# Delta-rule values transposed by VectorE and a trip through DRAM instead of by TensorE, and low parts of weights by an adding DMA, in a one-core decoder layer

## The chip, the core and the metric

The kernel runs on one core of a Trainium2 chip. The metric is the time of one execution on the device, in microseconds. Three runs of the kernel before took 1606.45, 1606.53 and 1606.76 us; the median is 1606.53 us.

## The reference

One layer of a decoder with 512 tokens of width 1024, all in float32: a half-weighted SwiGLU block (inner width 2816), a mixer, a second half-weighted SwiGLU block, and a final RMSNorm. The mixer projects its normalised input with one wide matrix and gives the columns to two branches: an HGRN2 branch (8 heads, columns called Q, F and B here) and a gated DeltaNet branch (8 key heads `k` and `q`, 16 value heads `v`, output gates `z`, and a few columns `D` for decays). The branches are projected back, merged by two gates (`t`), and projected once more. The change is in the DeltaNet branch, whose core is, for every value head and every chunk:

```python
cq, ck, cv = split(silu(causal_short_conv(concat(gq, gk, gv))))   # 4 taps along the tokens
u = T @ (v * beta[..., None])          # T: inverse of a unit lower triangular matrix of the chunk
w = T @ (kb * exp(gam)[..., None])
v_new = u_c - w_c @ S
o = (q_c * exp(gam_c)) @ S + qk_c @ v_new
S = S * exp(g_end) + k_to_end.T @ v_new
```

The convolution runs along the tokens, so its output is made with channels on the partitions; the recurrence multiplies `v` by matrices over tokens, so it wants tokens on the partitions. Between the two, each value head's block of 128 channels by 512 tokens has to be turned.

## The kernel before

**Tiling.** Activations lie transposed, channels on the 128 partitions and 512 tokens along the free axis. The kernel's chunk is 128 tokens, so there are NT = 4 chunks. Two value heads share a key head, and the kernel works on such pairs, `u` = 0 to 7.

**Precise products from pairs.** Weights and activations are split into a high part that TensorE's float32r format holds and a low remainder, and every product is three matmuls (`mm3`, L189 to L191: high by high, high by low, low by high). A weight slab is 128 x 512. In the mixer, SP loads it into one of three buffers `raw` (L1712), ScalarE copies it to `whi` (rounding, L1754), VectorE subtracts that from `raw` to give `wlo` (L1756), and TensorE uses both for four blocks of rows. There are six pairs of `whi` and `wlo` (WB = 6), three to each of two lanes that take turns. In the two SwiGLU blocks some slabs are done differently (L333 and L334): ScalarE writes minus the high part into `wlo`, and a DMA that GpSimd issues loads the weight from DRAM a second time and adds it into `wlo`.

**Stages.** The first SwiGLU block runs to about 360 us of the span, the mixer from there to about 1250, the second SwiGLU block to the end. Within the mixer the HGRN2 heads come first, then the DeltaNet pairs, and last a closing product `wbg` of the DeltaNet outputs, with the merge and the output projection.

**A planned order.** In the mixer, the order of instructions on every engine is fixed when the program is built. Each piece of work is a Python generator (a thread). It yields what it wants next: an engine for a reckoned time (`V(512)` is VectorE for 0.21 + 0.512 us, `A` is ScalarE, `T_` is TensorE, `S` is 0.4 us of SP), a pause (`lag`), a buffer (`get`), or events of other threads (`on`). The class `Desk` plays these against each other in reckoned time and writes down the instructions in the order that comes out; of the threads that are ready, the lowest rank goes first. Pieces marked `Patient` stand aside for up to 4 us (WAIT) while the dense products run. On the chip each engine then runs its list strictly in order, and waits where data or a buffer are not ready.

**The threads that matter here.**

- `loader` picks the next 128 columns to project from the list DENSE, as far as their buffers are free (`choose`), and loads their slabs. At most CONVS = 7 convolutions may be under way. If no column may be loaded it takes one of the 16 gate tiles `t`, as long as more than two are left; else it asks SP again after 0.5 us of reckoned time.
- `maker` turns a raw slab into its pair; `product` multiplies, in the order of loading.
- `conv` takes a projected k, q or v tile, scales it, applies the four taps (three steps of VectorE) and SiLU, and writes the result. For a value head that is L1113 into a buffer `vb`, channels on partitions.
- `g_w`, for each value head: four transposes of 128 x 128 on TensorE into a PSUM tile `ptv` (L1251), then a multiplication by per-token factors on VectorE (L1253) back into `vb`, now tokens on partitions.
- `g_n` and `g_b`: the pair's lower triangular blocks (eight products on VectorE, L1204); these go through DRAM to GpSimd, which inverts the 32 x 32 diagonal blocks in 31 dependent steps of two instructions (L1240, L1241).
- `g_inv` completes the inverse on TensorE; `g_rec` is the recurrence over the four chunks (L1374 to L1414), then normalisation, a transposition back (L1445) and the output gate. Pair `u` needs the inverse of `u`, and buffers that pair `u - 2` or an earlier one gives back.
- `operand` and, for the last two heads, the end of `g_rec` (L1458, L1460) split the outputs into pairs for the closing product, which uses heads 0 to 3 first and heads 12 to 15 last.

Of the kernel before, what the change touches and what calls it, by code (L numbers as in the profile page):

```python
# [8 lines left out]
F32 = mybir.dt.float32  # L9
# [3 lines left out]
ALU = mybir.AluOpType  # L13
# [3 lines left out]
P = 128  # L17
T = 512
# [30 lines left out]
STAY = (15,)  # L49
CONVS = 7  # L50
SLACK = 0.8
LAG = dict(raw=3.5, gb=6.5, nb=6, m=7, out=5, back=6)
EASE = 2.5
LANES = {"a": 2, "b": 2, "d": 1, "e": 1}

# [632 lines left out]
def mixer(tc, mp, e):  # L688
# [8 lines left out]
    def ps(name, lane="d"):  # L697
        return psc.tile([P, T], F32, tag="p" + lane, name=name, bufs=LANES[lane])

    def v3(ap, a):  # L700
        return ap.rearrange("p (a b) -> p a b", a=a)

    def bc(ap, n):

        return ap.unsqueeze(2).to_broadcast([ap.shape[0], ap.shape[1], n])
# [385 lines left out]
    def conv(k, i, pt, out, n):  # L1091

        yield "get", "ta", 2
        yield *V(512), 1
        ci = ta("ci", (P, T + 32))[:, :T + 3]
        dve.memset(ci[:, :3], 0.0)
        dve.tensor_tensor(ci[:, 3:], pt, rbc, op=ALU.mult)
        D.put("mm")
        wc = [cs[:, C_CV + 4 * i + j:C_CV + 4 * i + j + 1] for j in range(4)]
        yield A(512)  # L1100
        y = ta("cy")
        act.activation(y, ci[:, :T], AF.Copy, scale=wc[0])
        for j in range(1, 4):
            yield V(550)
            dve.scalar_tensor_tensor(y, ci[:, j:j + T], wc[j], y, op0=ALU.mult, op1=ALU.add)
        yield A(512)
        th = ci[:, :T]
        act.activation(th, y, AF.Tanh, scale=0.5)
        a, b = (v3(th, n), v3(y, n)) if n else (th, y)
        if k[0] in "qk" and k[1] > 3:  # L1110
            yield "on", ("K", k[1] - 4)
        yield V(512)
        dve.scalar_tensor_tensor(out, a, 1.0, b, op0=ALU.add, op1=ALU.mult)  # L1113
        D.put("ta", 2)
        D.fire(k)

    def g_e(u, st):

# [124 lines left out]

    def g_w(u, i, st):
        yield "on", ("v", 2 * u + i), ("C", u)
        yield "get", "e", 1
        vb = G["vb"][u % 3 * 2 + i]
        yield T_(Patient(.5))
        pt = ps("ptv", "e")
        for c in range(NT):  # L1250
            pe.transpose(pt[:, c * P:(c + 1) * P], vb[:, c], ident)  # L1251
        yield V(512)
        dve.tensor_tensor(vb, v3(pt, NT), bc(st["c2"][:, :, i], P), op=ALU.mult)  # L1253
        D.put("e")
        D.fire(("W", u, i))

    def g_inv(u, st):
# [75 lines left out]
    def g_rec(u, st):  # L1333
        yield "on", ("I", u), ("W", u, 0), ("W", u, 1), ("N", u), *([("R", u - 2)] if u > 1 else []), \
            *(["more"] if u else [("x", 0), ("we", 0), ("w", 0)])
        kq, kn, at, ut, sm = (st[k] for k in ("kq", "kn", "at", "ut", "sm"))
        vb = G["vb"][u % 3 * 2:u % 3 * 2 + 2]
        hd2 = [slice(i * P, (i + 1) * P) for i in range(2)]
        we, w, x = (G[n][u % 2] for n in ("we", "w", "x"))
        s = None  # L1340
# [27 lines left out]
        for c in range(NT):  # L1368
            pk = None
            if c > 0:  # L1370
                yield "get", "a", 1
                yield T_(.88)
                pk = ps("pks", "a")
                pe.matmul(pk[:, :256], kq[:, c, 0], s, start=True, stop=True)  # L1374
                pe.matmul(pk[:, 256:], kq[:, c, 1], s, start=True, stop=True)
                for i in range(2):
                    yield V(150)
                    dve.scalar_tensor_tensor(x[:, hd2[i]], pk[:, hd2[i]], st["c1"][:, c, i:i + 1], vb[i][:, c],
                                             op0=ALU.mult, op1=ALU.add)
                xs = [x[:, :P], x[:, P:]]  # L1380
            else:
                xs = [vb[0][:, c], vb[1][:, c]]
            yield "get", "b", 1
            yield T_(.46)
            pw = ps("pw", "b")
            for i in range(2):
                pe.matmul(pw[:, hd2[i]], ut[:, 4 * i + c], xs[i], start=True, stop=True)  # L1387
            D.start((2, u, c, 0), values(c, pw))
            if c < NT - 1:
                for i in range(2):  # L1390
                    yield V(150)
                    dve.tensor_scalar(we[:, hd2[i]], pw[:, hd2[i]], ek[:, c, 2 * u + i:2 * u + i + 1], None,
                                      op0=ALU.mult)
            yield "on", ("w", u, c)
            D.put("b")

            yield "get", "b", 1
            yield T_(.9)
            po = ps("pog", "b")
            if c < NT - 1:  # L1400
                pe.matmul(po[:, :256], kn[:, c], we, start=True, stop=True)
            for i in range(2):
                pe.matmul(po[:, 256 + i * P:256 + (i + 1) * P], at[i][:, c], w[:, hd2[i]], start=True, stop=True)  # L1403
            D.start((2, u, c, 1), outputs(c, po, pk))
            if c < NT - 1:
                yield "get", "s", 1
                s2 = places["s"]("s", (P, 256))
                if c == 0:
                    yield V(256)
                    dve.tensor_copy(s2, po[:, :256])  # L1410
                else:
# [284 lines left out]
    def loader():  # L1696
        n = 0
        while todo or gates:
            yield "get", "raw", 1
            x = choose()  # L1700
            while x is None:
                yield "use", "SP", 0.5
                x = choose()
            line.append(x)
            D.fire(("f", x))
            D.fire(("line", len(line)))
            for q, src in enumerate(weights(*x)):
                if q:
                    yield "get", "raw", 1
                yield S  # L1710
                raw = wp.tile([P, 512], F32, tag="raw", name="raw", bufs=RB)
                sp.dma_start(raw, src)  # L1712
                D.start((1, n), maker((x, q), raw))
                n += 1
        for d, q in wbgs:
            yield "get", "raw", 1
            yield S
            raw = wp.tile([P, 512], F32, tag="raw", name="raw", bufs=RB)
            sp.dma_start(raw, wbg[d][:, q * 512:(q + 1) * 512])
            D.start((1, n), maker((("m", d), q), raw))  # L1720
            n += 1

    def extra(n):
# [1 line left out]
        ab = op[4 + n]("wx", (P, 2, T), F32R)  # L1725
        return ab[:, 0], ab[:, 1]

    def maker(key, raw):
        yield "lag", LAG["raw"]
        (k, i), q = key  # L1730
        if k == "D":
# [20 lines left out]
            yield A(512)  # L1752
            lo, hi = e["pair"]()
        act.copy(hi, raw)  # L1754
        yield V(512)
        dve.tensor_tensor(lo, raw, hi.bitcast(F32), op=ALU.subtract)  # L1756
        D.put("raw")
        made[key] = hi, lo
        yield "lag", .4
        D.fire(("slab", key))  # L1760

    def product():
        for n in range(len(todo) + len(gates) + len(line)):
# [215 lines left out]
```

## Time and profile before

| | |
|---|---|
| median of three runs | 1606.53 us |
| profiled execution, span from first to last instruction | 1604.7 us |
| PE (TensorE matmul) busy | 1593.7 us, 99% |
| DVE (VectorE) busy | 1145.7 us, 71% |
| ACT (ScalarE) busy | 831.0 us, 52% |
| POOL (GpSimd) busy | 408.8 us, 25% |
| moved by DMA | 204.91 MB, 128 GB/s on average |
| of that, queue of GpSimd's DMAs | 26.22 MB |

The page gives the profiled execution's span and not its whole time; the median of the runs is 1.8 us above that span. PEld is TensorE's loading of weights, which overlaps its matmuls, and SPq is the queue of SP's DMA issues. In a row of a group, the names after the operation are output and inputs (buffer numbers left out), then shapes, then the count; behind the bar stand the busy time and the mean of one in ns, and after the next bar the idle time in front of it and what ended it. In a row of the timeline the first number is the start, the second the duration, both in us; brackets give the idle time before and what ended it.

### The profile page before, as it was taken

The numbers are of one execution on the slowest core, as the hardware profiler recorded it, in microseconds if no ns is written. First come the engines' busy times: TensorE is split into PE (matmuls) and PEld (weight loads), VectorE is DVE, ScalarE is ACT, GpSimd is POOL, SyncE is SP. The second block draws the span as 40 slices with busy tenths as digits, with TensorE's granted clock in tenths as the row PEclk, the third lists the DMA queues.
The fourth block names the chain that finished last, engine by engine and source line by source line (L and its number), as shares of the span: only waits on it lengthen the run. The fifth ranks groups of instructions, "written<-read, shape, count | busy, mean of one in ns | idle before, by whom it ended". The sixth has DMA issues, their size and how long they took to land.

```text
span 1604.7 us, 29242 instructions
## 1 busy us (share of the span) xinstructions
PE 1593.7 (99%) x10672; PEld 1386.3 (86%) x10672; DVE 1145.7 (71%) x2259; ACT 831.0 (52%) x1872; POOL 408.8 (25%) x725
## 2 busy tenths in 40 slices
PE   9999999999999999999999999999999999999997
PEld 8999998888888888888888888888888899999887
DVE  6888785447787778668788888765545788878433
ACT  5766674332434345456665665554324666667222
POOL 0211212001221221156545556600001121121001
PEclk9999999999999999999999999999999999999998
DMA  5766863332312322443242334445543586686333
GB/s 187 168 162 156 181 160 103 113 117 86 106 47 68 86 92 87 137 135 104 93 125 80 119 107 129 134 136 186 164 142 128 140 183 158 154 187 146 92 91 117
DMA packets 121824, 204.91 MB, mean 128 GB/s; under 512 B 21184, under 2 KB 27072, under 8 KB 121680
## 3 DMA queue, kind: packets, MB, share of 16 engines
q1 hardware_dynamic: 104688, 172.40, 34.3%
q0 software_dynamic: 14400, 26.22, 10.2%
q10 hardware_dynamic: 2592, 4.42, 1.0%
q8 instruction: 84, 1.38, 0.4%
q14 instruction: 60, 0.49, 0.1%
HBM read 188.02 MB, written 14.97 MB: 126 GB/s over the span
## 4 chain that ended last, share of the span: by engine, by line
PE 91%; DMA 3%; issue 3%; DVE 2%; ACT 0%; POOL 0%; POOLq 0%; SPq 0%; DVEq 0%; ACTq 0%
PE pmm L189 19%; PE pmm L191 19%; PE pmm L190 19%; PE px L191 6%; PE px L190 6%; PE px L189 6%; DMA wlo<-w1a 2%; PE pnat L189 2%; PE pnat L191 2%; PE pnat L190 2%; PE pgq L1189 1%; PE pw L1387 1%; PE pog L1403 1%; PE pl L974 1%; PE pd L917 1%
## 5 line engine op out<-in xcount | busy, mean ns | idle before, releaser
L189 PE MATMUL pmm<-uh,whi 128*128 128x512 f32 x879 | 361.3, 411 | 0.0
L191 PE MATMUL pmm<-uh,wlo 128*128 128x512 f32 x879 | 343.0, 390 | 0.0
L190 PE MATMUL pmm<-ul,whi 128*128 128x512 f32 x879 | 341.9, 389 | 0.0
L191 PE MATMUL px<-xs,wlo 128*128 128x256 f32 x1008 | 285.7, 283 | 1.3 <-DMA wlo<-w1a 0.7
L190 PE MATMUL px<-xs,whi 128*128 128x256 f32 x1008 | 285.2, 283 | 0.0
L189 PE MATMUL px<-xs,whi 128*128 128x256 f32 x1008 | 285.2, 283 | 0.0
L1754 ACT CAST whi<-raw 128x512 fp32r<-128x512 f32 x226 | 140.2, 621 | 242.7 <-PE pmm L190 195.2
L1756 DVE TENSOR_TENSOR wlo<-raw,whi 128x512 fp32r<-128x512 f32 x226 | 158.3, 702 | 118.2 <-ACT whi L1754 116.2
L191 PEld LDWEIGHTS pmm<-uh,wlo 128*128 128x128 f32 x879 | 165.0, 188 | 36.1 <-DVE wlo L607 0.2
L191 PEld LDWEIGHTS px<-xs,wlo 128*128 128x128 f32 x1008 | 193.5, 192 | 2.1 <-DMA wlo<-w1a 1.1
L189 PEld LDWEIGHTS px<-xs,whi 128*128 128x128 f32 x1008 | 193.5, 192 | 0.1
L190 PEld LDWEIGHTS px<-xs,whi 128*128 128x128 f32 x1008 | 193.5, 192 | 0.1
L189 PEld LDWEIGHTS pmm<-uh,whi 128*128 128x128 f32 x879 | 165.5, 188 | 30.4
L190 PEld LDWEIGHTS pmm<-ul,whi 128*128 128x128 f32 x879 | 165.7, 189 | 29.5 <-DVE ul L216 0.2
L329 ACT CAST whi<-sw 128x512 fp32r<-128x512 f32 x144 | 87.6, 613 | 92.8 <-DVE sw L366 72.6
L308 DVE TENSOR_TENSOR wlo<-raw,whi 128x512 fp32r<-128x512 f32 x100 | 77.7, 788 | 76.7 <-ACT whi L329 76.3
L329 ACT CAST whi<-raw 128x512 fp32r<-128x512 f32 x104 | 61.2, 592 | 125.6 <-PE pmm L190 92.8
L227 POOL TENSOR_TENSOR acc<-acc,sqt 128x512 f32<-128x512 f32 x18 | 23.4, 1302 | 319.8 <-ACT sqt L225 319.8
L308 DVE TENSOR_TENSOR wlo<-sw,whi 128x512 fp32r<-128x512 f32 x144 | 98.0, 681 | 0.0
L329 ACT CAST whi<-rw 128x512 fp32r<-128x512 f32 (+1 forms) x130 | 79.6, 613 | 26.6 <-PE px L190 13.4
L190 PE MATMUL pmm<-xs,whi 128*128 128x512 f32 (+1 forms) x238 | 89.7, 377 | 0.1
L189 PE MATMUL pmm<-xs,whi 128*128 128x512 f32 (+1 forms) x238 | 89.8, 377 | 0.0
(476 smaller groups left out, 3223.5 us busy)
## 6 DMA issues: line engine op xcount, KB each, us to landing
raw<-wt SPq DMA_DIRECT2D x160, 256.0 KB
rw<-w1b SPq DMA_DIRECT2D x80, 256.0 KB
rw<-w1a SPq DMA_DIRECT2D x74, 256.0 KB
wlo<-w1b POOLq DMA_DIRECT2D x53, 256.0 KB, 4.8
wlo<-w1a POOLq DMA_DIRECT2D x47, 256.0 KB, 5.0
raw<-w2b SPq DMA_DIRECT2D x41, 256.0 KB
raw<-w2a SPq DMA_DIRECT2D x36, 256.0 KB
raw<-wn SPq DMA_DIRECT2D x32, 256.0 KB
```

The lines of the kernel that those rows point to most:

```text
L189: pe.matmul(pt, ah, bh, start=first, stop=False)
L190: pe.matmul(pt, ah, bl, start=False, stop=False)
L191: pe.matmul(pt, al, bh, start=False, stop=last)
L227: add.tensor_tensor(acc, acc, s, op=ALU.add)
L308: dve.tensor_tensor(lo, x, hi.bitcast(F32), op=ALU.subtract)
L329: act.copy(hi, x)
L917: pe.matmul(pd[c // 2][:, (c % 2) * 192:(c % 2) * 192 + 192], ke[:, c * P:(c + 1) * P], qq[:, c], start=True, stop=True)
L974: pe.matmul(pl_[s0:s0 + 32, c * 16:(c + 1) * 16], ke[:, c * P + s0:c * P + s0 + 32], qv[:, c, r, :, 1], start=True, stop=True)
L1189: pe.matmul(pq[:, (c % 2) * 256:(c % 2) * 256 + 256], kq[:, c, 0], kq[:, c].rearrange("p a b -> p (a b)"), start=True, stop=True)
L1387: pe.matmul(pw[:, hd2[i]], ut[:, 4 * i + c], xs[i], start=True, stop=True)
L1754: act.copy(hi, raw)
L1756: dve.tensor_tensor(lo, raw, hi.bitcast(F32), op=ALU.subtract)
```

## The change

Two things change in the mixer.

**Turning the values.** For a value head, `conv` now writes its result to its own scratch tile `y`, and VectorE transposes it within blocks of 32 x 32 (`turn`) into the scratch tile `th`. `bounce` writes that tile to DRAM (256 KB) and reads it back in four transfers of 64 KB, one per 32 channels, each of which places the blocks so that tokens lie on partitions in `vb`. `g_w` then only multiplies, in place and from SBUF. In `vb` the columns are now ordered by block of 32 channels, then chunk, then channel, and `g_rec` reads them through a rearranged view. The two scratch tiles are given back at different times.

**Folded slabs.** Of every two slabs of a k, q, v or z tile, the second gets its low part as the SwiGLU blocks do: ScalarE writes the negated high part, and a DMA issued by GpSimd loads the weight again and adds it. The buffer `raw` is given back before that DMA.

Beside these, a loader that finds nothing to load asks again after 0.2 us of reckoned time rather than 0.5, behind all other work for SP.

```diff
-LAG = dict(raw=3.5, gb=6.5, nb=6, m=7, out=5, back=6)
+LAG = dict(raw=3.5, gb=6.5, nb=6, m=7, out=5, back=6, turn=2.5, fold=4.5)
...
         yield V(512)
-        dve.scalar_tensor_tensor(out, a, 1.0, b, op0=ALU.add, op1=ALU.mult)
-        D.put("ta", 2)
+        if n:
+            dve.scalar_tensor_tensor(out, a, 1.0, b, op0=ALU.add, op1=ALU.mult)
+            D.put("ta", 2)
+        else:
+            dve.scalar_tensor_tensor(y, a, 1.0, b, op0=ALU.add, op1=ALU.mult)
+            yield V(512)
+            turn(th, y)
+            D.put("ta")
+            yield from bounce(f"vn{i}", th, out, "ta")
         D.fire(k)
+
+    def turn(out, x):
+
+        dve.transpose(out.rearrange("p (f c j) -> p c f j", f=4, c=NT), x)
+
+    def bounce(name, x, out, tag=None):
+
+        yield S
+        scr = dr.tile([P, T], F32, name=name)
+        sp.dma_start(scr, x)
+        yield "lag", LAG["turn"]
+        if tag:
+            D.put(tag)
+        for f in range(4):
+            yield S
+            sp.dma_start(out[32 * f:32 * f + 32].rearrange("p (r a) -> p r a", r=4),
+                         scr.rearrange("(r i) (f a) -> f i r a", i=32, f=4)[f])
+        yield "lag", LAG["turn"]
...
     def g_w(u, i, st):
         yield "on", ("v", 2 * u + i), ("C", u)
-        yield "get", "e", 1
-        vb = G["vb"][u % 3 * 2 + i]
-        yield T_(Patient(.5))
-        pt = ps("ptv", "e")
-        for c in range(NT):
-            pe.transpose(pt[:, c * P:(c + 1) * P], vb[:, c], ident)
+        vb = G["vb"][u % 3 * 2 + i].rearrange("p r (c j) -> p r c j", c=NT)
         yield V(512)
-        dve.tensor_tensor(vb, v3(pt, NT), bc(st["c2"][:, :, i], P), op=ALU.mult)
-        D.put("e")
+        dve.tensor_tensor(vb, vb, st["c2"][:, :, i].unsqueeze(1).unsqueeze(3).to_broadcast([P, 4, NT, 32]), op=ALU.mult)
         D.fire(("W", u, i))
...
-        vb = G["vb"][u % 3 * 2:u % 3 * 2 + 2]
+        vb = [x.rearrange("p r (c j) -> p c r j", c=NT) for x in G["vb"][u % 3 * 2:u % 3 * 2 + 2]]
...
-                    dve.scalar_tensor_tensor(x[:, hd2[i]], pk[:, hd2[i]], st["c1"][:, c, i:i + 1], vb[i][:, c],
+                    dve.scalar_tensor_tensor(v3(x[:, hd2[i]], 4), v3(pk[:, hd2[i]], 4), st["c1"][:, c, i:i + 1], vb[i][:, c],
                                              op0=ALU.mult, op1=ALU.add)
...
             while x is None:
-                yield "use", "SP", 0.5
+                yield "use", "SP", 0.2, 20
                 x = choose()
...
         act.copy(hi, raw)
-        yield V(512)
-        dve.tensor_tensor(lo, raw, hi.bitcast(F32), op=ALU.subtract)
-        D.put("raw")
+        if folded(k, q):
+            yield A(512)
+            act.mul(lo, hi.bitcast(F32), -1.0)
+            D.put("raw")
+            yield "use", "POOL", .9
+            pool.dma_start(lo, src, accum_op=ALU.add)
+            yield "lag", LAG["fold"]
+        else:
+            yield V(512)
+            dve.tensor_tensor(lo, raw, hi.bitcast(F32), op=ALU.subtract)
+            D.put("raw")
+            yield "lag", .4
         made[key] = hi, lo
-        yield "lag", .4
         D.fire(("slab", key))
+
+    def folded(k, q):
+        return k in 'kqvz' and q % 2
```

Left out are the lines that hand the slab's source to `maker`.

More of the change, by code (lines that the diff above doesn't have):

```diff
@@ L1712, in loader @@
                 sp.dma_start(raw, src)
-                D.start((1, n), maker((x, q), raw))
+                D.start((1, n), maker((x, q), raw, src))
                 n += 1
@@ L1719, in loader @@
             sp.dma_start(raw, wbg[d][:, q * 512:(q + 1) * 512])
-            D.start((1, n), maker((("m", d), q), raw))
+            D.start((1, n), maker((("m", d), q), raw, wbg[d][:, q * 512:(q + 1) * 512]))
             n += 1
@@ L1726, in extra, with maker @@
         return ab[:, 0], ab[:, 1]
-    def maker(key, raw):
+    def maker(key, raw, src=None):
         yield "lag", LAG["raw"]
```

## The prediction

> **What bounds the kernel now.** I read the header and the engine table of the page, then TensorE's list of waits, then the busy time of each engine by stretch, and last the order of starts on TensorE around a transpose that goes.
>
> ```profile
> span 1604.7 us, 29242 instructions
> ...
> PE 1593.7 (99%) x10672; PEld 1386.3 (86%) x10672; DVE 1145.7 (71%) x2259; ACT 831.0 (52%) x1872; POOL 408.8 (25%) x725
> ```
> ```profile
> PE pbc L654 <- POOL rl L252: 1.1, 1, 1.1
> ```
> ```profile
> 100.00:200.00 100.00, 100.00 (x836) 100.00 (x835) 82.02 (x145) 63.74 (x123) 20.18 (x24) 1.00 0.73 167
> 900.00:950.00 50.00, 50.00 (x330) 41.52 (x329) 43.74 (x102) 33.35 (x102) 29.95 (x67) 1.00 0.37 116
> ```
>
> TensorE is busy for 1593.7 of 1604.7 us. Its list of waits (total, times, longest) has five rows, this one the longest, and none lies in the mixer. In the stretches (length, PE, PEld, DVE, ACT, POOL, clock, DMA share, GB/s) the delta rule's 900 to 950 has TensorE at 50 of 50, VectorE at 43.7, ScalarE at 33.4, GpSimd at 30.0. Since the end of a matmul is modelled, a wait could hide in it; so I look at starts:
>
> ```profile
> 667.80 0.39 PE L191 MATMUL pmm<-oh,wlo 128*128 128x512 f32 x1
> ...
> 670.52 0.39 PE L191 MATMUL pmm<-oh,wlo 128*128 128x512 f32 x1
> 670.75 0.60 PE L1251 MATMUL ptv<-sq,gvb 128*128 128x128 f32 x4
> 671.11 0.48 PE L189 MATMUL pmm<-oh,whi 128*128 128x512 f32 x1
> 671.42 0.39 PE L190 MATMUL pmm<-oh,whi 128*128 128x512 f32 x1
> ```
>
> Twelve steps lie between 667.80 and 670.52: 0.227 us from start to start, though each matmul "lasts" 0.39. The queue is really dense, and the cost of a matmul is its step. **TensorE's own work sets the time**; another engine matters only where it makes TensorE wait.
>
> **The change, part by part.** *The transposes.*
>
> ```profile
> L1251 PE MATMUL ptv<-sq,gvb x48: 270/272/330, 670.8 to 1027.7; 128*128 128x128 f32 x48
> L1251 PE MATMUL ptv<-sq,x x16: 272/272/328, 779.1 to 967.7; 128*128 128x128 f32 x16
> ```
>
> 64 transposes go, four for each of 16 heads. By durations that would be 64 x 0.272 = 17.4 us, but they overlap their neighbours. By starts, 670.52 to 671.42 holds two dense steps (0.453) and one head's four transposes: 0.90 - 0.453 = 0.447 us. Rounded down to 0.44, for heads that stand beside other small matmuls: 16 x 0.44 = **7.0 us less on TensorE**. The first chunk's L1387 now reads its values in runs of 32 with gaps: 16 small matmuls, at nothing because count and shape stay; at some 2 us in all if the gaps cost half of a 0.27 us matmul.
>
> *VectorE, ScalarE, GpSimd.* The rows give count, busy time and mean ns, or least, median and most ns.
>
> ```profile
> L1756 DVE TENSOR_TENSOR wlo<-raw,whi 128x512 fp32r<-128x512 f32 x221 | 155.0, 702 | 112.5 <-ACT whi L1754 110.5 <-PE pw L1387 0.6
> ...
> L1253 DVE TENSOR_TENSOR gvb<-ptv,sm 128x512 f32<-128x512 f32 x12 | 8.2, 681 | 2.0 <-PE ptv L1251 2.0
> ...
> L1272 DVE STREAM_TRANSPOSE h<-x 32x256 f32<-32x256 f32 x8 | 3.5, 435 | 0.2
> ...
> L1265 DVE STREAM_TRANSPOSE x<-gln 128x256 f32<-128x256 f32 x3 | 2.1, 701 | 0.0
> ```
> ```profile
> L333 ACT ACTIVATE wlo<-whi x100: 631/632/637, 39.4 to 1462.6; 128x512 fp32r<-128x512 f32 x100
> ```
> ```profile
> L334 POOL DMA_DIRECT2D wlo<-w1b x53: 853/862/929, 1256.4 to 1463.8; - x53
> ...
> DMA to landing us min/median/max: 3.8/4.8/7.8
> ```
>
> The k, q, v and z columns are 48 tiles of two slabs, so 48 subtractions leave VectorE: 48 x 0.702 = 33.7 us. Sixteen transposes of 128x512 come, a size without a row. The 256-wide ones take 0.435 (L1272) or 0.701 (L1265, scattered), so I bound it by 0.44 and twice 0.70, and take twice 0.435, as the new one reads in order like L1272: 14 us, at most 22. The multiplication stays at about 0.7 (L1253 from PSUM, L1756 from SBUF alone). VectorE is relieved by 20 us, at least 11. ScalarE gets 48 x 0.632 = 30 us, GpSimd 48 x 0.862 = 41 us, over some 400 us in which the stretch above leaves them a third and two fifths free.
>
> The Trainium skill ("VectorE: DVE Perf Modes", Rules for kernel authors) speaks against this part: a 128x128 transpose belongs on TensorE if PSUM will do as its destination. By duration the trace agrees, 0.45 us a head against 0.87 and a DMA trip; by that rule the sum would be a loss, which is rival C below.
>
> Does the longer way of a slab show?
>
> ```profile
> ACT whi L1754 <- PE pmm L190: 108.5, 101, 3.4
> ```
>
> ScalarE's slab copy mostly waits for a buffer that TensorE gives back, so the six pairs are full, and a new slab is wanted five slabs later: 5 x 12 x 0.227 = 13.6 us. Copy 0.62, negation 0.63 and landing 4.8 make 6.1 us, 9.1 with the longest landing: hidden, at nothing. Without this cover each folded slab would cost about its 6 us, against 1.3 of a plain one.
>
> *The trip through DRAM.* SP issues five more transfers per head, 80 in all; its first read waits for the write, and the loads of raw slabs stand behind it, for which ScalarE waits. The plan allows 2.5 us; the nearest row, a 256 KB transfer with addition, has 3.8 to 7.8. So SP stands 1 to 5 us per head, and I take 2. The multiplication waits for the reads in the same way, with the recurrence's small VectorE steps behind it; VectorE's idle 6 us in 50 and the 20 us of relief take up 16 x 2 us. Traffic grows by 80 x 256 KB = 21 MB, 52 GB/s on top of 116; at 167 (100 to 200 above) TensorE is still full. All this I cost at nothing; its other end is rival C.
>
> *The end of the mixer*, where the cover is thin. The chain on GpSimd (L1240, L1241) and the recurrence behind it must be over before the closing product needs the last head.
>
> ```profile
> 1010.25 0.26 POOL L1240 TENSOR_TENSOR fm<-gfs,gln 128x31 f32<-128x31 f32 x1 [11.77 <-DMA gln<-hmask]
> ...
> 1040.90 0.20 POOL L1241 TENSOR_TENSOR gln<-gln,fm 128x8 f32<-128x8 f32 x1
> ```
> ```profile
> 1123.11 0.60 PE L1445 MATMUL pto<-sq,on 128*128 128x128 f32 x4
> ...
> 1131.73 0.39 PE L189 MATMUL pmm<-uh,whi 128*128 128x512 f32 x1
> ```
> ```profile
> 1125.47 0.69 DVE L1460 TENSOR_TENSOR ul<-on,uh 128x512 fp32r<-128x512 f32 x1
> ```
>
> Head 15's operand is written at 1126.2. Counted from the start of the closing product, TensorE's matmul at 1131.73 is the first to use it: 5.6 us to spare. With 7.0 us less work TensorE arrives at 1124.7, so **what is late next** is this operand, by 1.4 us, if the recurrence ends where it does. Does it? One fold comes per tile, about every 8 us, so four fall into a GpSimd chain of 31 us (1010.25 to 1041.1): +3.4 us a chain. Against that:
>
> ```profile
> 674.87 0.25 POOL L1240 TENSOR_TENSOR fm<-gfs,gft 128x30 f32<-128x30 f32 x1
> ...
> 675.55 0.58 POOL L1240 TENSOR_TENSOR fm<-gfs,gft 128x29 f32<-128x29 f32 x1
> ```
> ```profile
> 927.93 0.78 DVE L1204 SCALAR_TENSOR_TENSOR gn<-gm,sm,x 128x128 f32<-128x128 f32 x2
> ...
> 946.83 1.48 DVE L1204 SCALAR_TENSOR_TENSOR gn<-gm,sm,x 128x128 f32<-128x128 f32 x5
> ```
>
> The 0.58 is an instruction that ran beside a slab subtraction on VectorE, the 0.25 one that did not: four subtractions fewer give a chain back some 1.3 us. (The Trainium skill, "GPSIMD Engine Reference", Key points, has GpSimd share its SBUF interfaces with VectorE and contend with instructions of two SBUF inputs; the trace agrees, 0.25 to 0.58.) And the eight products that feed the next chain are split by 18 us of other VectorE work, of which the relief, 20 us for eight pairs of heads, gives back 2.5 a pair. So +3.4 - 1.3 - 2.5: about nothing. I take an unmoved end, with 7 us earlier and 15 later as bounds.
>
> **The sum**: 1604.7 - 7.0 + 1.4 = 1599.1 for the profiled execution. The page gives its span only; the runs' median is 1606.53, so 1.8 us lie around the span: 1600.9.
>
> **The rivals.**
>
> *B, GpSimd becomes the bound, slower.* A fold holds GpSimd for 0.86 us and also while it waits for ScalarE's negation, which stands behind copies that wait up to 3.4 us for TensorE. The last two chains, of 31 us like the one above, carry some 7 folds. If each holds GpSimd for 1.9 us, less the 0.33 of a subtraction not met, the end moves by 7 x 1.57 = 11 us and the closing product waits it out: 1600.9 + 11 = 1612. It is slower by 0.2% from 1.6 us a fold (7 x 1.27 = 9). For it: GpSimd carries the only long serial chain, and each fold makes it meet an engine that TensorE paces. Against it: the plan puts each issue after the time it reckons for the negation.
>
> *C, slabs come late.* The two values of a pair bounce close together; then SP may stand 2 x 5 us, and with a folded slab's 9.1 that is 19 against 13.6 of cover: 5.5 us for each of 8 pairs, 44 at worst. I price a quarter: 1600.9 + 11 = 1612. It is slower by 0.2% once SP stands for 4.3 us a trip (8 x (8.6 + 6.1 - 13.6) = 9). For it: the load of the next slab stands in the same queue as the bounce. Against it: the median landing of 4.8 leaves 2.3 us a trip. (The Trainium skill, "DMA: Bandwidth & Descriptors", Anatomy of one DMA, has a wait sit on the issuing sequencer before dispatch; by that, all behind it stands too, which no run here shows yet.)
>
> *D, no net change.* If the recurrence is already the bound, TensorE's 7 us turn into a wait at the closing product: 1606 to 1607. For it: the loader takes a gate tile only when no projection may be loaded, and did so amid the delta rule:
>
> ```profile
> 997.14 0.68 DVE L1479 TENSOR_TENSOR tg<-pmm,rbc 128x512 f32<-128x512 f32 x1
> ```
>
> Against it: 5.6 us to spare.
>
> **How the numbers follow.** 0.2%, 3.2 us, is about what a measurement of this kernel can tell from no change. Forecast (1599 to 1603.3): 0.54. D: 0.17. B: 0.17. C: 0.12. So faster 0.54, same 0.17, slower 0.29. The likeliest is 1600.9. Downwards the range needs the full 7.0 with no stall and 1 us of unknowns, 1598.5; upwards it takes in D and the prices of B and C, to 1613, which leaves out their worse half, some 0.15. The forecast's own range is 1598.5 to 1603.3.
>
> **What would show it.** No L1251 in the trace, and TensorE's starts still 0.227 apart between 650 and 1030; a wait of 1 to 2 us of TensorE on the last operands of the closing product; VectorE some 20 us less busy, ScalarE 30 more. B would show GpSimd waiting on the negation and its chains over 36 us; C TensorE waiting on slabs and SP on the bounce's write; D a closing wait near 7 us. Wrong altogether if TensorE waits in the middle of the delta rule for something that stands in no row here.

## The result, and the profile after

The changed kernel took 1613.99 us (median of six runs, 1610.8 to 1618.68) against 1606.51 of the kernel before in the same session: the ratio is 1.0047, 95% interval 1.0036 to 1.0058. It is slower by half a per cent, where 1600.9 had been forecast. The profiled execution took 1610.8 us, the lowest of the six, and has a span of 1609.0; it lies 3.2 us below the median, and what follows is read from it.

The profile of the changed kernel, header and engine table:

```profile
span 1609.0 us, 29388 instructions
...
PE 1590.0 (99%) x10608; PEld 1378.9 (86%) x10608; DVE 1128.4 (70%) x2227; ACT 859.7 (53%) x1920; POOL 453.7 (28%) x773
```

The forecast sums of the engines came nearly true: 64 matmuls fewer, VectorE 17 us less busy, ScalarE 29 and GpSimd 45 more. Where is the time? The mixer lies between two broadcasts on TensorE. Before, they start at 363.27 and 1251.22, 887.95 us apart; after, the timeline of TensorE has:

```profile
362.76 1.05 PE L1881 MATMUL pbc<-sq,rcol 128*128 128x128 f32 x8
...
1254.93 1.05 PE L243 MATMUL pbc<-sq,rcol 128*128 128x128 f32 x8
```

That is 892.17 us: 4.2 more where 7.0 less were expected, so 11.2 us are lost inside the mixer, and the rest of the span is as it was. TensorE's list of waits after (total, times, longest) has five rows in the mixer, where the kernel before has none. The two costliest stand first:

```profile
PE pgq L1214 <- DVE gqm L1220: 3.5, 2, 3.2
PE pks L1393 <- DVE s L1433: 2.1, 1, 2.1
PE pbc L654 <- POOL rl L252: 1.1, 1, 1.1
...
PE pog L1420 <- DVE gwe L1411: 1.0, 2, 0.6
```

Both wait for small steps of VectorE, a masked product of 0.4 us and an update of the state of 0.35. Why were they late? VectorE's list and SP's, from 640 to 1060 us, rows with the trip through DRAM:

```profile
DVE gvb L1273 <- DMA gvb<-vn: 26.2, 10, 5.5
DVE x L1273 <- DMA x<-vn: 1.7, 2, 1.4
```
```profile
SPq L1138 <- DMA vn<-ci: 20.0, 10, 4.0
```

VectorE stood 28 us in front of the multiplication (L1273), and SP 20 us in front of the reads. One such place, on SP, VectorE and TensorE in turn:

```profile
672.05 0.43 SPq L1132 DMA_DIRECT2D vn<-ci  x1
...
675.51 1.74 SPq L1138 DMA_DIRECT2D gvb<-vn  x4
```
```profile
675.92 0.42 DVE L1218 TENSOR_TENSOR gm<-pgq,sq 128x256 f32<-128x256 f32 x1
679.05 0.69 DVE L1273 TENSOR_TENSOR gvb<-gvb,sm 128x512 f32<-128x512 f32 x1 [2.71 <-DMA gvb<-vn]
679.66 0.42 DVE L1220 TENSOR_TENSOR gqm<-pgq,sq 128x256 f32<-128x256 f32 x1
```
```profile
676.66 0.39 PE L191 MATMUL pmm<-oh,wlo 128*128 128x512 f32 x1
680.23 2.04 PE L1214 MATMUL pgq<-h 128*128 128x256 f32 x4 [3.18 <-DVE gqm L1220]
681.71 0.99 PE L189 MATMUL pmm<-oh,whi 128*128 128x512 f32 x1
682.50 0.63 PE L190 MATMUL pmm<-oh,whi 128*128 128x512 f32 x1
```

The write goes out at 672.05, the reads at 675.51, the multiplication runs at 679.05: 7.0 us, where the plan allows 2.5 for each half. L1220, whose input had long been there, stands behind the multiplication; it frees the PSUM tile that TensorE needs at L1214, and all dense products of the queue stand behind that. The chain of waits of the changed kernel has the same two pieces:

```profile
672.05 3.40 DMA vn<-ci
...
676.82 2.11 DMA gvb<-vn
679.05 0.12 DVE gvb L1273
```

The wait is dearer than it is listed. Until 683.70 the matmuls step by 0.79, 0.42, 0.43 and 0.35 us in place of 0.227, and L1214's four take 1.48 (680.23 to 681.71) in place of some 0.67: 1.9 us more. The windows (length, PE, PEld, DVE, ACT, POOL, clock, DMA share, GB/s) show why:

```profile
660.00:676.00 16.00, 16.00 (x76) 13.26 (x75) 6.90 (x15) 8.26 (x26) 4.28 (x9) 1.00 0.62 190
676.00:680.00 4.00, 1.04 (x5) 0.53 (x3) 1.29 (x5) 0.62 (x1) 3.22 (x11) 1.00 0.68 205
680.00:682.00 2.00, 1.77 (x5) 1.51 (x5) 0.68 (x2) 0.00 (x0) 1.76 (x4) 0.54 0.41 124
682.00:684.00 2.00, 2.00 (x7) 1.56 (x6) 1.69 (x6) 0.00 (x0) 0.31 (x1) 0.60 0.36 122
684.00:690.00 6.00, 6.00 (x28) 4.98 (x27) 3.16 (x8) 2.35 (x4) 3.19 (x7) 1.00 0.57 127
```

After the idle time the granted clock is 0.54 and 0.60, and 1.00 again from 684. By starts, against dense steps, this one place costs some 5.2 us, the one at 1010 (2.13 us listed, behind a stand of 4.94 us of VectorE) 2.4, and five smaller ones (0.3 to 0.6 us listed) some 2.9 together: 10.5 of the 11.2 us. Of the five, one, at 880 us, is right behind a stand of VectorE for the trip (2.65 us); two lie beside the HGRN2 heads, before any value head is turned.

### The profile page after: what moved, and what is told of

It reads as the page before. It is cut to its first block, busy times and chain, and to the rows that moved or that the text cites. A ratio compares the mean times of both kernels' runs of the same rounds, so it can differ in the third digit from the quotient of the medians.

```text
span 1609.0 us, 29388 instructions
## 1 busy us (share of the span) xinstructions
PE 1590.0 (99%) x10608; PEld 1378.9 (86%) x10608; DVE 1128.4 (70%) x2227; ACT 859.7 (53%) x1920; POOL 453.7 (28%) x773
## 4 chain that ended last, share of the span: by engine, by line
PE 84%; DMA 7%; issue 4%; DVE 3%; ACT 0%; SPq 0%; POOL 0%; POOLq 0%; DVEq 0%; ACTq 0%
PE pmm L189 18%; PE pmm L191 18%; PE pmm L190 18%; PE px L191 5%; PE px L190 5%; PE px L189 5%; DMA wlo<-w1a 2%; DMA wlo<-w1b 2%; PE pnat L189 2%; PE pnat L190 2%; PE pnat L191 2%; PE pgq L1214 1%; PE pog L1422 1%; PE pw L1406 1%; DMA gvb<-vn 1%
## 5 line engine op out<-in xcount | busy, mean ns | idle before, releaser
L1783 DVE TENSOR_TENSOR wlo<-raw,whi 128x512 fp32r<-128x512 f32 x178 | 125.1, 703 | 102.5 <-ACT whi L1773 94.3
L308 DVE TENSOR_TENSOR wlo<-raw,whi 128x512 fp32r<-128x512 f32 x100 | 77.7, 787 | 77.3 <-ACT whi L329 76.9
L334 POOL DMA_DIRECT2D wlo<-w1b x53 | 45.8, 864 | 168.8 <-ACT wlo L333 118.1
L189 PE MATMUL pmm<-xs,whi 128*128 128x512 f32 (+1 forms) x238 | 89.8, 377 | 0.0
```

The costliest lines, as they stand in the source:

```text
L189: pe.matmul(pt, ah, bh, start=first, stop=False)
L308: dve.tensor_tensor(lo, x, hi.bitcast(F32), op=ALU.subtract)
L334: pool.dma_start(lo, units[i].fold, accum_op=ALU.add)
```

## The experiments

**Theory V**: VectorE works in order; where it stands for the landing of the trip, the recurrence's small steps stand too, and TensorE with them. **Rivals**: SP's standing delays slabs and reads (S); the added traffic itself slows engines or transfers (C); the new order of the work is worse by itself (O); the folds, not the trip, do the harm (F). These letters are not those of the prediction's rivals. In the texts written before the runs, V is at first called W, and L is its wider form: a plan that reckons too little for a transfer makes some engine stand, and TensorE behind it. Only in the run without folds at 6 us does V stand for something else, VectorE's load. Ratios are to the kernel before, run between on the same chip (medians 1606.2 to 1606.55).

### Which part does it

*Without folds*: `folded` returns False, the trip stays.

```diff
     def folded(k, q):
-        return k in 'kqvz' and q % 2
+        return False
```

> The changed kernel with every slab's low part made by VectorE as before; values still turned by VectorE and through DRAM. Theory W (the wait for the DRAM trip is the cause: VectorE stands at the multiplication for reads that land later than the 2.5 us the plan allows, and TensorE stands behind it): VectorE's waits on the reads stay at 20 to 35 us, TensorE's at 5 to 12 us, time 1608 to 1618. Theory F (the folded slabs are the cause: GpSimd stands for ScalarE's negation, the chain on GpSimd gets longer, the inverses come late): without them the 7 us come through, 1599 to 1602. Theory O (the order of work that the plan happens to come to is the cause): anything from 1600 to 1615, with TensorE's waits at other places than at the instructions behind the multiplication.

1620.22 us, ratio 1.0088 [1.0073, 1.0103]. The trip alone costs more than both parts, and more than any of the three theories gave; F's 1599 to 1602 is far off. VectorE stands for the landing 16.5 us, less than the 20 to 35 expected. Of TensorE's two longest waits one (2.9 us, at L1214) comes after such a stand (1.7 us) and 2.6 us of other VectorE work. The other (3.4 us, at L1406) is behind VectorE, which waits 5.3 us for a slab copy of ScalarE; and ScalarE stood for the same trip, for a scratch tile that the write still holds. Its first wait on a transfer from 640 to 1060:

```profile
ACT cy L1102 <- DMA vn<-ci: 7.6, 1, 7.6
```

*Folds alone*: the kernel before with the folded slabs and the loader's new way of asking, values turned on TensorE.

```diff
+        if folded(k, q):
+            yield A(512)
+            act.mul(lo, hi.bitcast(F32), -1.0)
...
+            pool.dma_start(lo, src, accum_op=ALU.add)
+            yield "lag", LAG["fold"]
```

> The kernel before with only the folded slabs (and the loader's shorter pause); values turned by TensorE. Theory W: no DRAM trip, so TensorE hardly waits in the mixer and the time is that of before, 1605.5 to 1608. Theory F: GpSimd waits 40 to 60 us for ScalarE as in the changed kernel, TensorE waits 7 to 12 us, time 1612 to 1618. Theory O: 1605 to 1612.

1613.43 us, ratio 1.0047 [1.0031, 1.0063], in F's range: the folds alone do harm as well, by the same pattern on another engine. In the waits of ScalarE and of TensorE:

```profile
ACT sogb L1541 <- DMA og<-od: 3.9, 1, 3.9
```
```profile
PE pgq L1189 <- DVE gqm L1195: 3.0, 1, 3.0
```

ScalarE stands 3.9 us for a tile that the kernel had parked in DRAM; VectorE and then TensorE stand behind. That transfer was there before; only the order of the work around it is new.

*The loader's way of asking alone*, in the kernel before:

```diff
-                yield "use", "SP", 0.5
+                yield "use", "SP", 0.2, 20
```

> The kernel before with only the loader's pause changed (0.2 us, behind all other work of SP): no fold, no trip through DRAM, another planned order. Theory O (any other order costs some us): 1608 to 1615 with waits of TensorE in the mixer. Theory W, and its wider form L (a plan that reckons too little for transfers makes an engine stand in its order, and TensorE behind it): nothing that lands late is added, so 1605.5 to 1607.5 and no wait of TensorE in the mixer over 0.5 us.

1606.44 us, ratio 0.9999 [0.9990, 1.0008], and no wait of TensorE in the mixer. This edit costs nothing.

### Reckoning the landing longer

*6 us for each half of the trip.*

```diff
-LAG = dict(raw=3.5, gb=6.5, nb=6, m=7, out=5, back=6, turn=2.5, fold=4.5)
+LAG = dict(raw=3.5, gb=6.5, nb=6, m=7, out=5, back=6, turn=6, fold=4.5)
```

> The changed kernel with one number changed: the plan reckons 6 us instead of 2.5 for the write to DRAM and again for the reads. Theory W: the multiplication is put later in VectorE's order and the reads later in SP's; VectorE's waits on the reads fall from 28 to under 8 us, SP's on the write from 20 to under 8, TensorE's waits in the mixer to under 3 us, time 1599 to 1603. Theory F: waits of GpSimd and time stay, 1610 to 1616. Theory O: another order, 1603 to 1613, not tied to the waits on the reads.

1606.57 us, ratio 1.0001 [0.9992, 1.0010]: 7.4 us less than the changed kernel, but 3.6 above the range that W gave, with the same traffic (160 GB/s from 800 to 900, after 163). VectorE's stand falls from 28 to 1.9 us, SP's from 20 to 1.3. But the kernel only comes back to the time before, and a wait of TensorE at 810 us (1.9 us listed for L1168, and 0.5 just behind it) has come: in the new order ScalarE has a slab's copy and negation and six smaller copies ahead of the last of the squares (L1175) that free TensorE's tile. Behind it the clock is 0.50 and 0.65 for 4 us; by starts, from 808.28 to 815.52, the place costs some 4.4 us.

*6 us for the reads alone*, 2.5 for the write:

```diff
-LAG = dict(..., turn=2.5, fold=4.5)
+LAG = dict(..., turn=2.5, land=6, fold=4.5)
...
-        yield "lag", LAG["turn"]
+        yield "lag", LAG["land"]
```

> The changed kernel with 6 us reckoned for the reads alone; the write keeps 2.5 us. Theory W with the wait on VectorE as the harm: most of the gain of reckoning 6 us for both, 1600 to 1604, though SP still stands some 20 us for the write. If SP's standing, with the raw slabs behind it, is the harm instead: little changes, 1608 to 1615. Theory F: 1610 to 1616.

1613.38 us, ratio 1.0048 [1.0033, 1.0063], no gain, and the time that was given for SP's stand as the harm. SP now stands 32.6 us for the writes, so the reads go out late and VectorE still stands 12.6 us. That is less than half of the 28 us before, at the same time of the kernel: the sum of the stands is not the price. TensorE's longest wait is 2.1 us, at 836 us, for a step of VectorE (L1411) that runs 2.7 us after a multiplication that stood 2.4; the clock is 0.50 for some 6 us behind it.

*6 us a half, and 9 for the tile parked in DRAM* (`back`).

```diff
-... back=6, turn=2.5, fold=4.5)
+... back=9, turn=6, fold=4.5)
```

> The changed kernel with 6 us reckoned for each half of the trip and 9 instead of 6 for reading the DeltaNet outputs back. Theory L: the last engine that stood for a late transfer in the mixer is relieved too; 1600 to 1605. Theory O: 1603 to 1610, not tied to it. If the remaining 6 us of e3_turn6 against the forecast come from elsewhere (small waits of TensorE where a folded slab's columns begin, the plan's slots), 1605 to 1607 as e3_turn6.

1612.87 us, ratio 1.0039 [1.0024, 1.0054], a miss of all three ranges. TensorE waits 3.3 us at L1406, since VectorE stood for the trip at another instruction, the scaling of a gate tile (L1498) whose scratch tile the write still holds:

```profile
994.89 0.69 DVE L1498 TENSOR_TENSOR tg<-pmm,rbc 128x512 f32<-128x512 f32 x1 [4.85 <-DMA vn<-ci]
```

A longer reckoning is not better by itself; each gives another order, and the trip can be stood for in several places.

*6 us a half without folds*:

```diff
-... turn=2.5, fold=4.5)
+... turn=6, fold=4.5)
...
-        return k in 'kqvz' and q % 2
+        return False
```

> The changed kernel without folded slabs and with 6 us reckoned for each half of the trip. Theory L: the trip's waits vanish from VectorE and the time falls from the 1620 of e1_no_fold to 1601 to 1608. Theory V (without the folds VectorE is too full for the transposes as well, and it is that load and not the wait that cost 14 us): stays at 1614 to 1622.

1608.78 us, ratio 1.0016 [1.0007, 1.0026], just above L's range; VectorE stands for the landing only 0.5 us. With the trip reckoned at 6 us, the folds are worth 2 us (1606.57 with them).

*Folds alone, `back` at 9*:

```diff
-LAG = dict(raw=3.5, gb=6.5, nb=6, m=7, out=5, back=6)
+LAG = dict(raw=3.5, gb=6.5, nb=6, m=7, out=5, back=9, fold=4.5)
... (the other lines as for the folds alone)
```

> Folded slabs only, with 9 instead of 6 us reckoned for reading the DeltaNet outputs back, where e2_fold_only's longest wait of TensorE came from (ScalarE stood 3.9 us for that read). Theory L: 1605.5 to 1609. Theory F (the folds themselves, through GpSimd): 1611 to 1618 as e2_fold_only.

1610.39 us, ratio 1.0026 [1.0017, 1.0035], between the two ranges. ScalarE's stand of 3.9 us is gone with 3 us of the time; waits of 0.2 to 0.4 us remain, three beside the HGRN2 heads at 595 to 615 us and three in the closing product.

*6 us a half, folds only for v and z*, so that none lies beside the HGRN2 heads:

```diff
-        return k in 'kqvz' and q % 2
+        return k in 'vz' and q % 2
```

> The changed kernel with 6 us reckoned for each half of the trip, and folded slabs only for v and z, 32 instead of 48: the slabs of k and q go by subtraction, so that nothing folded lies beside the HGRN2 heads at 590 to 615. Theory L (what is lost are waits that the reckoned times made; the 7 us of TensorE are there): the three waits of 0.3 to 0.7 us at 590 to 615 go, 1600 to 1605 us, below the kernel before. Rival F (folding is what makes room on VectorE, and with less of it small waits come elsewhere, as in the kernel without folds at 1608.8): 1606.5 to 1609 us.

1606.76 us, ratio 1.0003 [0.9994, 1.0011]. The waits beside the HGRN2 heads went, as expected, and others of 0.3 to 1.0 us came elsewhere: rival F's time.

### The wait taken away, the order kept

*Without a reader*: the trip is made and nobody uses what it brings. The values are not turned for the recurrence, so the output is not the layer's; only the time is of use.

```diff
+    dump = mp.tile([P, T], F32, name="dump")
...
-            dve.scalar_tensor_tensor(y, a, 1.0, b, op0=ALU.add, op1=ALU.mult)
+            dve.scalar_tensor_tensor(out, a, 1.0, b, op0=ALU.add, op1=ALU.mult)
             yield V(512)
-            turn(th, y)
+            turn(th, out)
             D.put("ta")
-            yield from bounce(f"vn{i}", th, out, "ta")
+            yield from bounce(f"vn{i}", th, dump, "ta")
```

> The changed kernel in its own order, but nobody reads what the trip through DRAM brings: the result of a value head goes straight into its buffer, VectorE transposes it into the scratch tile, that is written to DRAM and read back into a tile which no instruction uses, and the multiplication works on values that were not turned. The traffic, SP's waits for the writes and every instruction on VectorE stay; only VectorE's wait for the landing goes. Theory V (VectorE, standing in order at the multiplication, makes TensorE wait): the idle time of the multiplication falls from 26 to about 0 us, TensorE's waits of 3.2 and 2.1 us in the delta rule go, and the time is 1601 to 1605 us. Rival S (it is SP's stand that delays slabs and reads): SP still stands about 20 us, and the time stays at 1609 to 1614. Rival C (the traffic itself): 1610 to 1614.

1602.76 us, ratio 0.9978 [0.9968, 0.9987]: 11.2 us below the changed kernel, in the same order of work on every engine (8.0 us between the two profiled executions, 7.4 of it at the two places at 680 and 1010). Its lists: SP's first row, then TensorE's rows of the mixer, the only ones that it has.

```profile
SPq L1139 <- DMA vn<-ci: 21.3, 11, 3.8
```
```profile
PE pl L981 <- DVE fl L994: 0.9, 1, 0.9
...
PE pk L1008 <- ACT hkn L1013: 0.4, 1, 0.4
PE pl L975 <- DVE ah L939: 0.3, 1, 0.3
```

SP stands as long as in the changed kernel, and that costs nothing that can be seen. The three waits left are those beside the HGRN2 heads. S and C fall, for the loss of the changed kernel; so do O and F, since the order and the folds are still there.

*Traffic only*: the reads also take a tile that has long been written, so SP does not stand either.

```diff
... (the lines of the kernel without a reader)
+    first = []
...
         sp.dma_start(scr, x)
+        first.append(scr)
+        scr = first[0]
```

> As the kernel without a reader, and the reads also take their data from the first head's DRAM tile, which has long been written, so SP does not stand for the write either; the values are again not turned. All 21 MB of the trips move, but nothing waits for them save a scratch tile for its write. Theory V: no more than 1 us below the kernel without a reader, 1601 to 1604 us. Rival S: this is where the gain comes, 1601 to 1605 us against 1609 or more without a reader alone. Rival C (a DMA share near 0.6 slows slabs or engines by itself): 1609 to 1614 us in both.

1602.16 us, ratio 0.9973 [0.9962, 0.9984]: within 0.6 us of the one before. SP's 21 us are worth that at most, and the added 21 MB (8.4 of the trips, 12.6 of the folds) at a DMA share of 0.64 (700 to 800 us) cost nothing that shows.

### The wait moved, the values used

*The multiplication held back in the plan*, until GpSimd has inverted the pair's blocks:

```diff
-        yield "on", ("v", 2 * u + i), ("C", u)
+        yield "on", ("v", 2 * u + i), ("C", u), ("P", u)
```

> The changed kernel with one condition more: the multiplication of a pair's values waits in the plan until GpSimd has inverted that pair's diagonal blocks, some tens of us after the values were turned; the recurrence needs both anyway. All computed as in the changed kernel, with 2.5 us reckoned for each half of the trip and all the folds. Theory V (only VectorE's stand at the multiplication costs): its idle time on the landing falls from 26 us to under 3, no wait of TensorE above 1 us is left in the delta rule, and the time is 1600 to 1605 us, below the kernel before by 1 to 6 us as in the kernel without a reader. Rival O (every new order brings its own small waits, as 6 us reckoned did): 1606 to 1612 us, with the waits at other instructions than the multiplication.

1636.52 us, ratio 1.0184 [1.0170, 1.0198], a large miss of both ranges: VectorE still stands 23.5 us at the multiplication, in eight places. The two longest, from VectorE's list from 640 to 1060, and SP's timeline for the first:

```profile
DVE gvb L1273 <- DMA gvb<-vn: 9.9, 4, 8.3
DVE gvb L1273 <- DMA gln<-hmask: 6.9, 1, 6.9
```
```profile
911.68 2.50 SPq L1138 DMA_DIRECT2D gvb<-vn  x3
914.28 2.60 SPq L1253 DMA_DIRECT2D gfs<-nb  x4
916.92 0.46 SPq L1259 DMA_DIRECT2D gln<-hmask  x1
917.48 0.46 SPq L1731 DMA_DIRECT2D raw<-wt  x1
917.99 0.43 SPq L1138 DMA_DIRECT2D gvb<-vn  x1
```

The plan, which goes by rank, put six other transfers between a head's third read and its fourth, and VectorE stood 8.3 us for that head. The 6.9 us come about in the same way at 1017 us, and TensorE's longest wait, 5.8 us, is behind them. It is the same wait, longer; how the rest of the 30 us is made up was not taken apart.

*Only the multiplication moved*: the order of TensorE, ScalarE, GpSimd and SP is that of the changed kernel, instruction by instruction, and on VectorE the 16 multiplications stand four, or eight, planned turns later, at the latest in front of the pair's recurrence (`D.step(u)` there). Lines behind the edit have shifted: L1284 is the multiplication, L1424 is L1411, L1433 is L1420.

```diff
+            if e == "DVE":
+                self.step()
...
-        dve.tensor_tensor(vb, vb, ...)
+        D.late.append([9, u, lambda: dve.tensor_tensor(vb, vb, ...)])
         D.fire(("W", u, i))
```

(9 for eight turns, 5 for four; `step` counts down and issues what has reached zero.)

> The changed kernel with the order of TensorE, ScalarE, GpSimd and SP exactly as it is; on VectorE each of the 16 multiplications stands four planned VectorE turns later (some 3 us), and nothing else moves. All is computed. Theory V (VectorE's stand at the multiplication, with the recurrence's small steps behind it, is what TensorE waits for): the idle time on the landing falls from 28 us to about a third, TensorE's waits of 3.2 and 2.1 us shrink or go, and the time is 1603 to 1609 us. Rival D (in the kernel without a reader the gain came from data that nobody needed, since the values as such come too late): the recurrence waits for the later multiplication instead, 1610 to 1616 us.

> As the kernel moved by four turns, but by eight (some 6 us), at the latest in front of that pair's recurrence. Theory V: almost no idle time on the landing, no wait of TensorE above 1 us in the delta rule, and 1601 to 1605 us, as the kernel without a reader (1602.8), so below the kernel before by 0.1 to 0.3%. Rival D: not below 1609 us, with TensorE waiting at L1406 or L1393 of the recurrence for values multiplied too late.

By four turns 1605.0 us, ratio 0.9995 [0.9986, 1.0004]; by eight 1603.94 us, ratio 0.9989 [0.9980, 0.9998]. VectorE's stand falls from 28 us to 6.4 and 2.3. The groups of VectorE from 640 to 1050, after and with eight turns (busy, mean ns, idle in front):

```profile
L1273 DVE TENSOR_TENSOR gvb<-gvb,sm 128x512 f32<-128x512 f32 x12 | 8.5, 711 | 26.2 <-DMA gvb<-vn 26.2
```
```profile
L1284 DVE TENSOR_TENSOR gvb<-gvb,sm 128x512 f32<-128x512 f32 x12 | 8.4, 703 | 1.2 <-DMA gvb<-vn 1.2
```

And the same stretch as a window, after and with eight turns:

```profile
640.00:1050.00 410.00, 403.34 (x2497) 331.60 (x2496) 311.68 (x684) 266.51 (x734) 257.59 (x551) 1.00 0.62 163
```
```profile
640.00:1050.00 410.00, 408.34 (x2532) 336.82 (x2532) 318.15 (x697) 271.17 (x749) 254.62 (x551) 1.00 0.63 164
```

Same DMA share, same GB/s, some 5 us more work of TensorE. So the values do not come too late as such (rival D): moving 16 instructions of 0.7 us by some 6 us takes 10 us off the changed kernel. Of the kernels that compute the layer, the one with eight turns is the only one whose interval lies below the kernel before: by 0.1%, which is less than the 0.2% that the prediction took for what a measurement can tell, and the interval ends just below 1. TensorE's list has six waits left in the mixer of the kernel with eight turns, 3.0 us in all:

```profile
PE pog L1433 <- DVE gwe L1424: 1.7, 3, 0.8
...
PE pl L991 <- DVE fl L1004: 0.6, 1, 0.6
```

the other two (0.4 and 0.3) are beside the HGRN2 heads as well.

*6 us a half and moved by six turns*:

> The changed kernel planned with 6 us for each half of the trip, and the multiplications six VectorE turns later in that order. There VectorE stood for the landing only 1.9 us in all, and the loss was one wait of 2.4 us at 807 us, with another cause. Theory V: little is left to gain, 1605 to 1607.5 us. Rival M (moving the multiplications helps in any order, because VectorE's order as such is too eager): 1601 to 1604 us.

1606.7 us, ratio 1.0003 [0.9994, 1.0012], as without moving. Where VectorE hardly stands, moving gives nothing; the wait at 810 us is still there.

## Why the prediction was wrong, point by point

- **The 7.0 us on TensorE: right to some 0.5 us, by this reckoning.** The mixer takes 883.45 us without a reader (363.54 to 1246.99), 4.5 less than before, with three waits beside the HGRN2 heads listed at 1.55 us. By starts a wait costs some 0.16 us more than it is listed, since the modelled end of the matmul ahead lies behind its step; so they are worth some 2 us, and 0.5 is left for all else, the reads with gaps among it. No run takes these three waits away and keeps the rest.
- **The engines' sums: right, two sizes off.** A transposition took 0.707 us and not 0.87, a fold 0.89 of GpSimd and not 0.862. The comparison "0.45 us a head against 0.87", said to be by duration, sets TensorE's cost by starts beside a duration of VectorE; by duration a head's four transposes are 4 x 0.272 = 1.1 us against the 0.707 measured.
- **The folded slab's longer way, hidden: right for the slabs** (TensorE waits for none), but the folds change the order of the work, and alone they cost 7 us (a wait of 3.0 us with the clock behind it, and small ones), or 4 with 9 us reckoned for the parked tile (small ones only). No term of the sum stood for that.
- **The trip through DRAM: here it failed.** The step says that SP stands 2 us a head, that the multiplication waits in the same way, "with the recurrence's small VectorE steps behind it", that "VectorE's idle 6 us in 50 and the 20 us of relief take up 16 x 2 us", and then "All this I cost at nothing". The size was right: VectorE stood 28 us, 1.7 a head, SP 20 in ten times. The conclusion was not: the stand of an engine that works in order is not paid out of its idle time on average. It falls on what stands behind it at that moment, and here that is, at 680 us, a step of 0.4 us that holds a PSUM tile for which TensorE waits, and at 1010 an update of the state that TensorE reads. Most of the 12 stands fell where TensorE had other work; two did not, and with the clock behind the first they cost TensorE 7.6 us. In the profiled executions that is nearly all of the 8.0 us that the stand is worth; the medians lie 11.2 us apart, and where the other executions lost 3 us more no trace shows. Without the stand and with all else in place the time is 1602.8, or 1603.9 with the multiplications moved, against the 1600.9 forecast.
- **Its other end, rival C, came near the time for another reason.** 1612 was given for SP standing and slabs coming late. SP did stand, the slabs were not late, and the kernels without a reader and with traffic only differ by 0.6 us. The mechanism was the one set down as the sign of "wrong altogether": TensorE waiting in the middle of the delta rule.
- **Rival B was met in half of its sign.** GpSimd did stand for ScalarE, idle 77 us in all in front of the folds, but its last chain took 33.5 us (1010.32 to 1043.82) against 30.9 before, below the 36 named; no wait of TensorE leads to it.
- **The stall of 1.4 us at the closing product did not come**, even in the kernels that got 4.5 us ahead of the one before.
- **The prediction's rival D** (no net change through a closing wait) had no part.

The Trainium skill ("DMA: Bandwidth & Descriptors", Anatomy of one DMA) gives 2.0 us and the bytes at 436 GB/s for a transfer that GpSimd issues: 2.6 us as an estimate for 256 KB. The folds are 256 KB transfers of GpSimd that also add, and they landed in 3.7 to 7.0 us (median 4.8). The trip's write, which SP issues and which that figure is not given for, took 3.40 us in the chain above. No run here has either on an otherwise idle queue.

What stays open is why the runs of the changed kernel spread over 8 us where those of the kernel before spread over 1 to 3, and which order would give the full 7 us, since the kernels that fold k and q have waits beside the HGRN2 heads that the kernel before has not.

## What to carry to other kernels

A wait put on an engine that works in order is priced by what stands behind it at that place, down to the engine that sets the time, and not by the idle share of the engine that waits. In front of an instruction that waits for a transfer, look in the trace for the small steps behind it, and move the waiting instruction later in that engine's queue before changing anything else: 16 instructions moved by some 6 us were worth 10 us here, and nothing in an order where VectorE stood only 1.9 us. A plan's allowance for a transfer is checked against landings in the loaded stretch, and a longer allowance is tried for the whole order that it brings, since it may bring another wait.

## What the runs showed of the hardware

An idle time of TensorE can cost as much again in clock, and its length alone does not tell whether it will. After 3.18 us of idle time the granted clock was 0.54 and 0.60 for 4 us (above). In the kernel with folds alone, after 2.97 us, it was 0.50 for 8 us:

```profile
964.00:966.00 2.00, 1.47 (x4) 1.23 (x5) 2.00 (x6) 1.89 (x7) 1.69 (x5) 0.50 0.00 0
...
970.00:972.00 2.00, 2.00 (x7) 1.52 (x6) 1.48 (x3) 0.56 (x1) 1.76 (x5) 0.50 0.82 143
```

With 6 us reckoned for each half of the trip, 1.88 us before 810.86 were enough, with another 0.52 before 812.04:

```profile
812.00:814.00 2.00, 1.96 (x5) 1.58 (x6) 1.85 (x7) 1.86 (x9) 1.58 (x1) 0.50 0.85 204
814.00:816.00 2.00, 2.00 (x15) 1.34 (x15) 0.38 (x1) 0.23 (x2) 1.52 (x2) 0.65 0.52 172
```

In the kernel with the multiplication held back the clock stayed at 1.00 after 3.05 us, and in the changed kernel after 2.13. The Trainium skill ("TensorE: Matmul & The Clock Gate", Part 1) has the clock fall to half after at least one idle window of some 3.4 us, the windows running freely. The runs agree on the half, but not on the idle window: less idle time than that was enough in all three cases above where the clock fell. The short one stands beside 32 small matmuls (32x32, L1308); whether such matmuls count as work no run tells.

GpSimd's 0.89 us for issuing a fold and the higher DMA share, 0.62 after 0.37 from 640 to 1050 us, had no cost on TensorE that these runs can show: the kernel without a reader has both, and some 0.5 us of its mixer is all that is not put down to a listed wait.
